# Expert gates in a two-layer block: fp16 operands that hold two tokens interleaved instead of four

## The chip, the core and the metric

The kernel runs on one core of a Trainium2 chip, in one launch. A core has TensorE (PE: matmuls; PEld is its weight load, which overlaps the matmul), VectorE (DVE), ScalarE (ACT), GpSimd (POOL) and SyncE (SP, which issues DMAs). The metric is the device time of one execution in microseconds (us); the kernel before is given by the median of three runs, and the changed one is timed in the same way. One execution of each kernel was profiled, and all rows below come from that one.

## What is computed

The program is two transformer-like blocks on 256 tokens of width 1024. The change is in the last part of the second block, a feed-forward layer with 16,384 experts (PEER). Every token has 8 heads; each head picks 16 experts out of 128 x 128 by two lists of sub-keys, and gets a softmax gate for each. Cut to what matters:

```python
T = 256; PEER_HEADS = 8; PEER_TOPK = 16; PEER_NKEYS = 128
best_s, best_j = lax.top_k(cand_s, PEER_TOPK)
idx = jnp.take_along_axis(cand_i, best_j, axis=-1)   # expert = 128 * i1 + i2
gates = jax.nn.softmax(best_s, axis=-1)

def retrieve(args):
    xc, ic, gc = args
    uc = u_tab[ic]
    vc = v_tab[ic]
    hdn = jax.nn.gelu(jnp.einsum('cd,chkd->chk', xc, uc)) * gc
    return jnp.einsum('chk,chkd->cd', hdn, vc)
```

## The kernel before

The kernel gathers nothing. It computes all 128 x 128 experts for all tokens as dense products, row by row: a row is the 128 experts with one value of i1.

- **Values of the hidden layer.** For each of 128 rows, `row` multiplies the row of `u` with the tokens. Each row of weights (512 KB) is read by a DMA on SP's queue and split in two parts (`whi` by ScalarE at line 123, `wlo` by VectorE at line 124), and a product is three matmuls (lines 183 to 185), here with 128 x 128 weights and 256 moving columns in a 4-byte type into the tile `pu`. ScalarE applies Gelu (line 1628) and leaves the result in `H`, 128 (i2) x 128 rows (i1) x 256 tokens.
- **Gates.** `H` is then multiplied by a gate that is zero for all but the 128 chosen experts of a token. `gates(g, t0)` makes these factors for 8 tokens (`G`) and for one half (`g`) of the 128 rows. With a token's 128 choices on the partitions, `b` holds a one-hot of i2 (128 wide), `e` a one-hot of the half's 64 values of i1, and `a` is `e` times the gate, in a coarse part and a remainder (`k` = 0, 1). These are fp16 tiles made by VectorE (lines 1661, 1663 and, twice, 1666). For each token two fp16 matmuls (line 1670; weights from `b`, 128 x 128; moving operand from `a`, 64 columns) add up to the 128 x 64 factors in the PSUM tile `pw`; VectorE multiplies them into `H` (line 1672). So a block of gates is 16 pairs of weight load and matmul on TensorE and five VectorE operations, and there are 2 halves x 32 groups of tokens = 64 blocks, 1,024 such matmuls in all.
- **Output.** For each of 128 rows `hs` is the split of `H` (lines 1715 and 1716), and four groups of three matmuls (lines 183 to 185, 512 moving columns) add the row of `v` into four PSUM tiles `pout`.

Four tokens lie interleaved in the fp16 tiles: the last index of `b`, `e` and `a` is the token within its group of four, so that VectorE's operations have rows of four consecutive 2-byte elements. A token's slice, which TensorE reads, is then every fourth element: its columns are 8 bytes apart, in `a` (moving operand) and in `b` (weights) alike. The constant `iob` holds each number from 0 to 127 four times, to be compared with.

The order is set by the program text: `step` puts the next block of gates behind a pair of rows when the block is due or when a budget of VectorE time allows. The first half's blocks stand among the `pu` rows, the second half's among the `pout` rows. Every engine works through its own queue in order; `b` and `a` have two buffers each, `e` one, `pw` two.

Of the kernel before, what the change touches and what calls it, by code (L numbers as in the profile page):

```python
# [23 lines left out]
F16 = mybir.dt.float16  # L24
# [3 lines left out]
OP = mybir.AluOpType  # L28
# [3 lines left out]
P = 128  # L32
# [52 lines left out]
class K:  # L85
# [1515 lines left out]
    def peer(self, out, parked_x):  # L1601
        nc, tc, d = self.nc, self.tc, self.d

        AT = (0, 64, 128)
        G = 8
        with ExitStack() as ctx:
            pool = lambda n, b, **kw: ctx.enter_context(tc.tile_pool(name=self.name(n), bufs=b, reuse_waits="tile", **kw))
            pu = pool("ppu", 2, space=PSUM)
# [4 lines left out]
            wk = pool("pwk", 2)  # L1613
            i1b = keep.tile([P, S], F16, name="i1b")
            i2b = keep.tile([P, S], F16, name="i2b")
            g2 = keep.tile([P, 2, S], F16, name="g2")
            iob = keep.tile([P, P, 4], F16, name="iob")
# [34 lines left out]

            def gates(g, t0):

                n, r0 = G // 4, AT[g]
                nr = AT[g + 1] - r0
                t4 = lambda a: a[:, t0:t0 + G].rearrange("p (n t) -> p n t", t=4)
                b = wk.tile([P, n, P, 4], F16, name=self.name("b"), tag="b")
                e = wk.tile([P, n, 64, 4], F16, name=self.name("e"), tag="e", bufs=1)[:, :, :nr]
                a = wk.tile([P, 2, n, 64, 4], F16, name=self.name("a"), tag="a")[:, :, :, :nr]  # L1660
                nc.vector.tensor_tensor(b, t4(i2b).unsqueeze(2).to_broadcast([P, n, P, 4]),
                                        iob.unsqueeze(1).to_broadcast([P, n, P, 4]), op=OP.is_equal)
                nc.vector.tensor_tensor(e, t4(i1b).unsqueeze(2).to_broadcast([P, n, nr, 4]),
                                        iob[:, r0:r0 + nr].unsqueeze(1).to_broadcast([P, n, nr, 4]), op=OP.is_equal)
                for k in range(2):
                    nc.vector.tensor_tensor(a[:, k], t4(g2[:, k]).unsqueeze(2).to_broadcast([P, n, nr, 4]), e, op=OP.mult)
                pw = self.pw.tile([P, G, 64], F32, name=self.name("pw"), tag="pw")[:, :, :nr]
                for t in range(G):
                    for k in range(2):
                        nc.tensor.matmul(pw[:, t], b[:, t // 4, :, t % 4], a[:, k, t // 4, :, t % 4], start=k == 0, stop=k == 1)  # L1670
                hv = H[:, r0:r0 + nr, t0:t0 + G]
                nc.vector.tensor_tensor(hv, pw.rearrange("p t a -> p a t"), hv, op=OP.mult)

            def work():

                for c in self.route(keep, sc, room, iob, g2, i1b, i2b):
                    yield ROUTED, c
                for g in range(len(AT) - 1):
                    for t0 in range(0, S, G):
                        yield P - 1 + AT[g], GCOST[0] + GCOST[1] * (AT[g + 1] - AT[g]) / 64  # L1680
                        gates(g, t0)
# [47 lines left out]
            g = H[:, 8:12].rearrange("p a b -> p (a b)")  # L1729
# [44 lines left out]
def _plan(start, stop):  # L1774
# [41 lines left out]
    for n, f in ((1, lambda: ffn(0, 1)), (2, nsa), (3, lambda: (ffn(0, 2), ffn(1, 1))), (4, diff),  # L1816
                 (5, lambda: ffn(1, 2)), (6, block2), (99, peer)):
        if start < n <= stop:
            f()
# [172 lines left out]
```

## Time and profile before

| | us |
|---|---|
| median of 3 runs | 2266.61 (2261.97 to 2271.68) |
| the profiled execution, device time | 2267.65 |
| its span, first to last instruction | 2265.9 |
| TensorE busy | 2214.5 (98%) |
| VectorE busy | 1643.8 (73%) |
| ScalarE busy | 1137.3 (50%) |
| mean granted TensorE clock | 0.984 of full |

The profiled execution lies 1.04 us above the median, and 1.75 us of it are outside its span. Busy time counts an engine as busy while any of its instructions is running; matmuls overlap one another, so what a matmul costs in a stream is the distance from its start to the next one's start, not its own duration. The blocks of gates run from 1666.5 to 2049.4 us of the span.

### The profile page before, as it was taken

How to read it: one execution, taken by the hardware profiler on the slowest of the kernel's cores; microseconds unless marked ns; L12 is line 12 of the kernel's file. 1: busy time of each engine (PE TensorE's matmuls, PEld its weight loads, DVE VectorE, ACT ScalarE, POOL GpSimd, SP SyncE). 2: the span in 40 equal slices, each digit the busy share in tenths (PEclk: the TensorE clock that was granted, in tenths of full speed). 3: DMA queues.
4: the chain of work that ended last, by engine and by line, in shares of the span. 5: the costliest groups of instructions: out<-in, count | busy, mean ns of one | idle time of the engine just before them, and what ended most of it. 6: DMA issues, size and time to landing. Idle time of an engine off the chain costs nothing. (4 is left out here: it accounts for less than half of the span.)

```text
span 2265.9 us, 35790 instructions
## 1 busy us (share of the span) xinstructions
PE 2214.5 (98%) x13730; PEld 1875.1 (83%) x13730; DVE 1643.8 (73%) x3303; ACT 1137.3 (50%) x1789; POOL 33.3 (1%) x75
## 2 busy tenths in 40 slices
PE   8999999999999998999999999999999999999999
PEld 7887646888788776888787777999999998888887
DVE  6867666997787587787577567896767767885555
ACT  6554575554555464655455444454533344334443
POOL 1000000000000002000000000000000000000000
PEclk9999989999999997999999999999999999999999
DMA  6654424888655442555432125445544445445554
GB/s 215 195 190 170 154 70 148 298 272 269 237 198 182 166 150 74 163 190 193 130 138 85 66 85 194 140 168 195 184 161 149 150 167 186 159 155 180 195 194 150
DMA packets 107563, 383.33 MB, mean 169 GB/s; under 512 B 13440, under 2 KB 13824, under 8 KB 107392
## 3 DMA queue, kind: packets, MB, share of 16 engines
q1 hardware_dynamic: 103392, 374.39, 48.7%
q10 hardware_dynamic: 3360, 4.55, 0.6%
q8 instruction: 108, 1.77, 0.3%
q0 software_dynamic: 640, 2.11, 0.3%
q14 instruction: 63, 0.52, 0.1%
HBM read 378.89 MB, written 2.11 MB: 168 GB/s over the span
## 5 line engine op out<-in xcount | busy, mean ns | idle before, releaser
L123 ACT ACTIVATE whi<-raw 128x1024 fp32r<-128x1024 f32 x654 | 690.7, 1059 | 767.5 <-PE pout L184 205.0
L124 DVE TENSOR_TENSOR wlo<-raw,whi 128x1024 fp32r<-128x1024 f32 x654 | 797.7, 1223 | 327.1 <-ACT whi L123 318.7
L191 PE MATMUL pair<-xx,whi 128*128 128x512 f32 x1280 | 449.8, 396 | 0.0
L192 PE MATMUL pair<-xx,wlo 128*128 128x256 f32 x1280 | 359.8, 281 | 0.0
L183 PE MATMUL pu<-xx,whi 128*128 128x256 f32 x1024 | 292.6, 286 | 1.1 <-ACT H L1628 1.1
L184 PE MATMUL pu<-xx,wlo 128*128 128x256 f32 x1024 | 290.2, 283 | 0.0
L185 PE MATMUL pu<-xx,whi 128*128 128x256 f32 x1024 | 290.1, 283 | 0.0
L191 PEld LDWEIGHTS pair<-xx,whi 128*128 128x128 f32 x1280 | 240.8, 188 | 55.7 <-issue 0.2
L192 PEld LDWEIGHTS pair<-xx,wlo 128*128 128x128 f32 x1280 | 242.7, 190 | 0.5 <-issue 0.2
L183 PE MATMUL pout<-whi,hs 128*128 128x512 f32 x512 | 201.4, 394 | 0.2 <-ACT hs L1715 0.2
L184 PE MATMUL pout<-whi,hs 128*128 128x512 f32 x512 | 199.5, 390 | 0.2 <-DVE hs L1716 0.2
L185 PE MATMUL pout<-wlo,hs 128*128 128x512 f32 x512 | 199.6, 390 | 0.0
L183 PEld LDWEIGHTS pu<-xx,whi 128*128 128x128 f32 x1024 | 197.0, 192 | 1.3 <-ACT H L1628 1.3
L184 PEld LDWEIGHTS pu<-xx,wlo 128*128 128x128 f32 x1024 | 196.5, 192 | 0.0
L185 PEld LDWEIGHTS pu<-xx,whi 128*128 128x128 f32 x1024 | 196.4, 192 | 0.0
L183 PE MATMUL pair<-whi,hT 128*128 128x512 f32 x352 | 138.5, 393 | 6.6 <-DVE x L350 6.6
L185 PE MATMUL pair<-wlo,hT 128*128 128x512 f32 x352 | 139.2, 396 | 0.0
L184 PE MATMUL pair<-whi,lT 128*128 128x512 f32 x352 | 138.3, 393 | 0.0
L183 PE MATMUL bank<-whi,xx 128*128 128x512 f32 x288 | 118.0, 410 | 1.1 <-DVE rsg L167 0.5
L184 PE MATMUL bank<-whi,xx 128*128 128x512 f32 x288 | 115.7, 402 | 0.0
L185 PE MATMUL bank<-wlo,xx 128*128 128x512 f32 x288 | 114.9, 401 | 0.0
L185 PEld LDWEIGHTS pout<-wlo,hs 128*128 128x128 f32 x512 | 96.1, 188 | 20.2
(562 smaller groups left out, 3505.5 us busy)
## 6 DMA issues: line engine op xcount, KB each, us to landing
raw<-in_pu_dram SPq DMA_DIRECT2D x128, 512.0 KB, 3.5
raw<-in_pv_dram SPq DMA_DIRECT2D x128, 512.0 KB, 3.5
raw<-in_f1i_dram SPq DMA_DIRECT2D x88, 512.0 KB, 4.1
raw<-in_f2i_dram SPq DMA_DIRECT2D x88, 512.0 KB, 4.3
araw<-in_wada_dram SPq DMA_DIRECT2D x48, 512.0 KB, 4.7
raw<-in_f1o_dram SPq DMA_DIRECT2D x44, 512.0 KB, 3.5
raw<-in_f2o_dram SPq DMA_DIRECT2D x44, 512.0 KB, 3.7
raw<-in_wi_dram SPq DMA_DIRECT2D x28, 512.0 KB, 3.4
```

Source lines behind the costliest of these rows:

```text
L123: nc.scalar.activation(hi, raw, AF.Copy)
L124: nc.vector.tensor_tensor(lo, raw, hi.bitcast(F32), op=OP.subtract)
L183: mm(out, lh, rh, start=start, stop=False)
L184: mm(out, ll, rh, start=False, stop=False)
L185: mm(out, lh, rl, start=False, stop=stop)
L191: mm(out, lh, rr, start=start, stop=False)
L192: mm(out[:, 0], ll, rr[:, 0], start=False, stop=stop)
```

## The change

A new constant `Q = 2` takes the place of the 4 in the layout: `b`, `e` and `a` hold groups of two tokens. Their sizes are the same (four groups of two instead of two groups of four for 8 tokens). A token's slice is now every second element, columns 4 bytes apart. VectorE's operations have the same number of elements, in rows of two, and read the first two of the four copies in `iob`. The matmuls are the same in number and shape.

```diff
         AT = (0, 64, 128)
         G = 8
+        Q = 2
...
-                n, r0 = G // 4, AT[g]
+                n, r0 = G // Q, AT[g]
                 nr = AT[g + 1] - r0
-                t4 = lambda a: a[:, t0:t0 + G].rearrange("p (n t) -> p n t", t=4)
-                b = wk.tile([P, n, P, 4], F16, name=self.name("b"), tag="b")
-                e = wk.tile([P, n, 64, 4], F16, name=self.name("e"), tag="e", bufs=1)[:, :, :nr]
-                a = wk.tile([P, 2, n, 64, 4], F16, name=self.name("a"), tag="a")[:, :, :, :nr]
-                nc.vector.tensor_tensor(b, t4(i2b).unsqueeze(2).to_broadcast([P, n, P, 4]),
-                                        iob.unsqueeze(1).to_broadcast([P, n, P, 4]), op=OP.is_equal)
-                nc.vector.tensor_tensor(e, t4(i1b).unsqueeze(2).to_broadcast([P, n, nr, 4]),
-                                        iob[:, r0:r0 + nr].unsqueeze(1).to_broadcast([P, n, nr, 4]), op=OP.is_equal)
+                tq = lambda a: a[:, t0:t0 + G].rearrange("p (n t) -> p n t", t=Q)
+                b = wk.tile([P, n, P, Q], F16, name=self.name("b"), tag="b")
+                e = wk.tile([P, n, 64, Q], F16, name=self.name("e"), tag="e", bufs=1)[:, :, :nr]
+                a = wk.tile([P, 2, n, 64, Q], F16, name=self.name("a"), tag="a")[:, :, :, :nr]
+                nc.vector.tensor_tensor(b, tq(i2b).unsqueeze(2).to_broadcast([P, n, P, Q]),
+                                        iob[:, :, :Q].unsqueeze(1).to_broadcast([P, n, P, Q]), op=OP.is_equal)
+                nc.vector.tensor_tensor(e, tq(i1b).unsqueeze(2).to_broadcast([P, n, nr, Q]),
+                                        iob[:, r0:r0 + nr, :Q].unsqueeze(1).to_broadcast([P, n, nr, Q]), op=OP.is_equal)
                 for k in range(2):
-                    nc.vector.tensor_tensor(a[:, k], t4(g2[:, k]).unsqueeze(2).to_broadcast([P, n, nr, 4]), e, op=OP.mult)
+                    nc.vector.tensor_tensor(a[:, k], tq(g2[:, k]).unsqueeze(2).to_broadcast([P, n, nr, Q]), e, op=OP.mult)
...
-                        nc.tensor.matmul(pw[:, t], b[:, t // 4, :, t % 4], a[:, k, t // 4, :, t % 4], start=k == 0, stop=k == 1)
+                        nc.tensor.matmul(pw[:, t], b[:, t // Q, :, t % Q], a[:, k, t // Q, :, t % Q], start=k == 0, stop=k == 1)
```

No instruction is added, removed or moved: the instructions of all engines stand in the order in which they stood, and only the line numbers behind the new line are higher by one.

## Rows read from the trace of the kernel before

**Rows 1.** The page: busy time of each engine; the chain that ended last, by line.

```profile
PE 2214.5 (98%) x13730; PEld 1875.1 (83%) x13730; DVE 1643.8 (73%) x3303; ACT 1137.3 (50%) x1789; POOL 33.3 (1%) x75
...
PE pout L183 5%; PE pout L184 5%; PE pout L185 5%; PE pu L183 5%; PE pu L184 5%; PE pu L185 5%; PE pw L1670 3%; DVE wlo L124 1%; DVE H L1524 1%; DVE H L1526 0%; DVE H L1523 0%; DVE H L1525 0%; DVE H L1522 0%; PE pq L183 0%; PE pq L184 0%
```

**Rows 2.** Busy time by stretch: gates among pu rows, then among pout rows.

```profile
core 0: us, PE busy (x) PEld busy (x) DVE busy (x) ACT busy (x) POOL busy (x), PEclk, DMA share, GB/s
1666.50:1845.00 178.50, 178.50 (x1726) 177.46 (x1725) 134.22 (x211) 66.36 (x77) 0.00 (x0) 1.00 0.44 149
1880.00:2049.40 169.40, 169.04 (x1088) 140.07 (x1086) 143.94 (x229) 67.93 (x79) 0.00 (x0) 1.00 0.49 164
```

**Rows 3.** Chain of waits from 1660 us (start, us, what) and from 1880 us.

```profile
1759.17 1.00 PE pw L1670 x16
1760.17 0.17 PE pu L183
1765.97 1.01 PE pw L1670 x16
1766.98 0.17 PE pu L183
1772.79 2.00 PE pw L1670 x32
...
1946.34 1.00 PE pw L1670 x16
1947.35 0.28 PE pout L183
1952.87 1.01 PE pw L1670 x16
1953.88 0.28 PE pout L183
```

**Rows 4.** Timeline about one block: start, us, engine, line, what [idle before].

```profile
1765.33 0.28 PE L185 MATMUL pu<-xx,whi 128*128 128x256 f32 x1
...
1765.45 0.28 PE L183 MATMUL pu<-xx,whi 128*128 128x256 f32 x1
...
1765.81 0.99 PEld L1670 LDWEIGHTS <-b 128*128 128x128 f16 x16
1765.81 1.17 PE L1670 MATMUL pw<-a,b 128*128 128x64 f16 x16
...
1766.79 0.36 PE L183 MATMUL pu<-xx,whi 128*128 128x256 f32 x1
```

**Rows 5.** The same view among the pout rows.

```profile
1948.63 0.39 PE L183 MATMUL pout<-whi,hs 128*128 128x512 f32 x1
1948.86 0.39 PE L184 MATMUL pout<-whi,hs 128*128 128x512 f32 x1
...
1949.72 0.76 DVE L1666 TENSOR_TENSOR a<-g,e 128x512 f16<-128x512 f16 x2
...
1952.71 1.17 PE L1670 MATMUL pw<-a,b 128*128 128x64 f16 x16
```

**Rows 6.** The first two weight loads of the block of rows 4.

```profile
1765.81 0.15 PEld L1670 LDWEIGHTS <-b 128*128 128x128 f16 x2
```

**Rows 7.** Instructions of the gates: min/median/max ns, first and last start.

```profile
L1670 PEld LDWEIGHTS <-b x1024: 111/117/139, 1666.5 to 2048.9; 128*128 128x128 f16 x171
L1670 PE MATMUL pw<-a,b x1024: 227/243/251, 1666.5 to 2049.0; 128*128 128x64 f16 x171
```

**Rows 8.** VectorE by line and shape, 1560 to 2265 us: xcount | busy us, mean ns | idle before.

```profile
L124 DVE TENSOR_TENSOR wlo<-raw,whi 128x1024 fp32r<-128x1024 f32 x224 | 273.9, 1223 | 156.7 <-ACT whi L123 156.7
L1666 DVE TENSOR_TENSOR a<-g,e 128x512 f16<-128x512 f16 x128 | 48.8, 420 | 0.0
L1672 DVE TENSOR_TENSOR H<-pw,H 128x512 f32<-128x512 f32 x64 | 44.1, 690 | 54.3 <-PE pw L1670 54.3
L1661 DVE TENSOR_TENSOR b<-i2b,iob 128x1024 f16<-128x1024 f16 x64 | 43.9, 686 | 1.6 <-PE pw L1670 1.6
...
L1663 DVE TENSOR_TENSOR e<-i1b,iob 128x512 f16<-128x512 f16 x64 | 27.0, 422 | 1.1
...
L1588 DVE TENSOR_TENSOR H<-H 128x1024 f16<-128x1024 f16 x2 | 1.3, 668 | 0.0
```

## The prediction

> **What bounds the kernel now.** I read the page first: TensorE is busy 98% of the span, and the chain that ended last names it for every stage of the expert layer, with 3% of the span for the fp16 matmuls of the gates [rows 1]. The change touches nothing outside 1666.5 to 2049.4 us, so the question is what sets the pace there. The table by stretch shows TensorE busy without a gap in both parts, at the full granted clock (1.00, the 2.4 GHz level), while VectorE stands idle for 178.5 - 134.2 = 44.3 us of the first part and 25.5 us of the second, and ScalarE and the DMA engines are about half busy or less [rows 2]. The chain by time says the same from block to block: about 1.00 us of gate matmuls, then at once `pu` or `pout` matmuls; a double block takes 2.00 us, exactly twice one [rows 3]. VectorE waits for TensorE at the multiply into `H` (54.3 us over the 64 blocks, 0.85 us each), not the other way round [rows 8]. So a nanosecond taken from a gate matmul is a nanosecond of the span, as long as VectorE keeps up.
>
> **What a gate matmul costs, and why.** The sixteen matmuls of a block take 1.17 us from the first start to the last end; the last alone takes 0.243 (the median), so fifteen steps take 0.927 us, 62 ns each [rows 4, 7]. That is much for 64 columns. The 4-byte matmuls around them give a scale: with 256 columns they start 0.12 us apart [rows 4], with 512 columns 0.23 us apart [rows 5], with the same 128 x 128 weights. The difference, 0.11 us for 256 columns, is 0.43 ns a column, one tick of 2.4 GHz (0.417 ns) within the rounding; 13 ns are left over for each matmul (120 - 107). By that scale 64 columns cost 27 ns and a step 40 ns at most. The measured 62 ns is 22 more. Taking off the same 13 leaves 49 ns for 64 columns, and taking off nothing leaves 62: 1.8 to 2.3 ticks a column, in place of one.
>
> Is it the weight load that takes so long? The first two loads of a block, which have nothing before them in the block to wait for, are both done after 0.15 us, and one alone takes 0.111 to 0.117 us, so the second ended 0.033 to 0.039 us after the first [rows 6, 7]. A load can thus be repeated every 36 ns or so; that is not the 62. What differs between the gate matmuls and the others is the spacing of the moving columns: 4 bytes in `pu` and `pout`, where 4-byte elements lie side by side, 8 bytes in the gates. Twice the bytes passed over for a column, about twice the time. That is the reading on which the forecast rests: moving columns 4 bytes apart stream at one tick each, columns 8 bytes apart at two.
>
> **The change part by part.** *Moving operand.* Columns are 4 bytes apart, the spacing that streams at one tick in rows 4 and 5. The step should fall from 62 ns to 27 ns plus a leftover. The leftover is 13 ns in the `pu` rows and 62 - 53 = 9 ns in the gates themselves if their columns take two ticks. That gives 36 to 40 ns. The weight load is the next bound, at some 36 ns if its own spacing makes no difference to it, so the step can't fall much below that unless loads get faster too. I take 37 ns: the load's bound and the gates' own leftover agree on 36, and 40 pulls it up a little. No row shows 2-byte elements at a 4-byte spacing, so both ends stand for the range: 27 ns with no leftover at all, and 62 ns, no change. A step above 62 I exclude: the columns lie in half as many bytes as before, and nothing else of the matmul changes.
>
> *Sum on TensorE.* Each of the 64 blocks has 15 steps inside it, 960 in all; the step from the last matmul to the next `pu` or `pout` matmul I leave as it is, because there the 4-byte weights are being loaded (that matmul takes 0.36 us where its neighbours take 0.28 [rows 4]). 960 x (62 - 37) = 24.0 us. With 40 ns it is 21.1 us, with 36 ns 25.0 us, with 27 ns 33.6 us.
>
> *Weights.* `b`'s columns come closer too. Loads lie beside the matmuls, so a faster load gives nothing beyond what is counted; it only lifts the bound of 36 ns.
>
> *VectorE.* Five operations a block, same elements. The fp16 ones run at double pace: 422 ns for 512 elements and 686 for 1024, where the 4-byte ones take 690 and 1223 [rows 8]. Do rows of two keep that pace? The nearest row is the fp16 add of line 1588 on 1024 elements, in rows of 32: 668 ns, against 686 for `b` in rows of four. Eight times as many rows cost 18 ns at most, 0.08 ns a row. Doubling them for `b`, `e` and two `a` adds 640 rows, some 50 ns a block by that, and nothing that ends the wait: VectorE idles 44.3 / 32 = 1.38 us a block in the first part (32 blocks) and 25.5 / 30 = 0.85 us in the second (30 blocks lie inside that stretch, two just before it). I count it at nothing; the cover is that idle time. A gain below nothing I don't expect from rows twice as many. If it is gone, see the last rival.
>
> *What is late next.* With blocks 15 x 25 = 0.375 us shorter, VectorE's idle time falls to about 1.0 and 0.48 us a block, and its wait for `pw` shrinks by the same 0.375 us, since the multiply into `H` is what waited. The factors of a block are ready well ahead: `a` begun at 1949.72 and done 0.76 us later belongs to the block that starts at 1952.71, 2.2 us on [rows 5]. So TensorE doesn't start to wait. The DMA share of 0.44 to 0.49 rises by a fifteenth.
>
> *Time.* 2267.65 - 24.0 = 2243.6 us for the profiled execution. That one lay 1.04 us above the median, so against the median: 2266.61 - 24.0 = 2242.6, which I call 2243 us. Differences under about 0.5% (11 us) are what a measurement of this kernel can't tell from no change.
>
> **The rivals.**
> *Partial.* The cost could go by a column's place in memory in finer steps than two and one, or a floor for a pair of load and matmul could lie between 37 and 62 ns. For: the 49 to 62 ns are not a clean two ticks, and nothing shows 2-byte elements at 4 bytes. Against: 4-byte elements at that spacing are at full pace [rows 4, 5]. With a step of 50 ns the gain is 960 x 12 = 11.5 us: 2255. [...]
>
> *No gain.* The 62 ns is a fixed price of a pair whose weights are 2-byte, or the 8-byte spacing costs nothing and the columns are not what is slow: then 2266 to 2267. For: no other 2-byte matmul stands in the trace to compare with. Against: the loads' 33 to 39 ns [rows 6, 7] and one tick a column leave no resource that is busy for 62. [...]
>
> *Slower: VectorE loses its double pace.* If operands in rows of two are taken one element at a time, `b` goes from 686 to 1223 ns and `e` and both `a` from 421 to 690, together + 1.34 us a block [rows 8]. Among the `pu` rows that fits into 1.38 us of idle time and just eats the gain. Among the `pout` rows the idle time is 0.85 us a block: VectorE becomes the bound there, and a block's period grows by 1.34 - 0.85 = 0.49 us, 30 x 0.49 = 14.7 us. That gives 2281 us, and it decides from + 0.85 us a block. Against: the rows of four and of 32 cost the same, which says that row ends are not paid for; two elements still fill a pair.
>
> **How the numbers follow.** Forecast (steps of 27 to 43 ns, 2233 to 2249): 0.65. Partial: 0.13, half of it over 0.5%. No gain: 0.16. Slower: 0.05; 0.01 is left. Faster by over 0.5%: 0.65 + 0.07 + 0.02 for a small gain that chance helps over the line = 0.74; within: 0.06 + 0.14 + 0.01 = 0.21; slower: 0.05. The range holds the forecast and the partial case: from 960 x 34 = 33 us gained (2234) to 2264, where only the no-gain and the slower case are left out.
>
> **What would show it.** In the profile after, a block's sixteen matmuls should span 0.243 + 15 x 0.037 = 0.80 us in place of 1.17, and a double block some 1.2 us on the chain in place of 2.00; `pu` and `pout` steps stay at 0.12 and 0.23 us. VectorE's four fp16 operations should keep 686 and 421 ns, within 30; its wait for `pw` should fall from 54 to about 30 us. I am wrong if the block still spans 1.1 us or more (column spacing is not the price), if TensorE shows idle time or steps over 62 ns in front of `H`'s rows, or if `b` takes over 1 us.

## The result

The changed kernel takes 2235.52 us (median of 4 runs, 2227.63 to 2239.65) against 2264.29 us for the kernel before in the runs beside it (2259.22 to 2271.68): a ratio of 0.9866, interval 0.9825 to 0.9908, some 29 us or 1.3% faster. The forecast was 24 us, 2243. The direction held, and the cause that was named is borne out by the experiments; the gain is a fifth larger than forecast, because the step between gate matmuls was put too high, and the time lies at the very edge of the range (2234 to 2264).

The profiled execution of the changed kernel has a span of 2237.8 us against 2265.9, 28.1 us less. Its lines beside those of before, first the gates' instructions by tile (min/median/max ns; first and last start), to be compared with [rows 7]:

```profile
L1671 PEld LDWEIGHTS <-b x1024: 96/97/101, 1669.0 to 2020.9; 128*128 128x128 f16 x171
L1671 PE MATMUL pw<-a,b x1024: 191/193/205, 1669.0 to 2021.0; 128*128 128x64 f16 x171
```

The stretch from the first gate matmul to the last shrank from 382.5 us (1666.5 to 2049.0) to 352.0, 30.5 us less. That is a little more than the whole gain: this execution came to the gates 2.5 us later than the one before, through stages that the change doesn't touch. The timeline about one block (start us, us, engine, line, what), to be compared with [rows 4]:

```profile
1720.97 0.28 PE L185 MATMUL pu<-xx,whi 128*128 128x256 f32 x1
1721.09 0.54 PEld L1671 LDWEIGHTS <-b 128*128 128x128 f16 x16
1721.10 0.66 PE L1671 MATMUL pw<-a,b 128*128 128x64 f16 x16
...
1721.59 0.36 PE L183 MATMUL pu<-xx,whi 128*128 128x256 f32 x1
...
1721.79 0.28 PE L184 MATMUL pu<-xx,wlo 128*128 128x256 f32 x1
```

Sixteen matmuls span 0.66 us in place of 1.17. With 0.193 us for the last alone, a step is (0.66 - 0.193) / 15 = 31 ns, where it was 62. The chain of waits shows the same, blocks of 0.50 us and double blocks of 0.99 in place of 1.00 and 2.00 [rows 3]:

```profile
1714.44 0.99 PE pw L1671 x32
1715.43 0.20 PE pu L183
1721.25 0.50 PE pw L1671 x16
1721.75 0.20 PE pu L183
```

VectorE by line and shape (xcount | busy us, mean ns | idle before), beside [rows 8]: the operations in rows of two take what the rows of four took, and the wait for `pw` has fallen from 54.3 to 30.7 us.

```profile
L1667 DVE TENSOR_TENSOR a<-g,e 128x512 f16<-128x512 f16 x128 | 48.8, 419 | 0.0
L1673 DVE TENSOR_TENSOR H<-pw,H 128x512 f32<-128x512 f32 x64 | 44.0, 689 | 30.7 <-PE pw L1671 30.7
L1662 DVE TENSOR_TENSOR b<-i2b,iob 128x1024 f16<-128x1024 f16 x64 | 43.8, 685 | 1.1 <-PE pw L1671 1.1
```

Busy time by stretch (PE, PEld, DVE, ACT, POOL, granted clock, DMA share, GB/s), beside [rows 2]: the DMA share rises from 0.44 and 0.49 to 0.51 and 0.55, twice the fifteenth that was forecast, and VectorE has 164.00 - 134.04 = 29.96 us of idle time left among the `pu` rows (32 blocks, 0.94 us each) and 153.60 - 141.88 = 11.72 among the `pout` rows (30 blocks, 0.39 us each). The forecast had 1.0 and 0.48.

```profile
1669.00:1833.00 164.00, 164.00 (x1735) 162.94 (x1734) 134.04 (x211) 66.69 (x77) 0.00 (x0) 1.00 0.51 164
1867.40:2021.00 153.60, 153.54 (x1081) 125.08 (x1081) 141.88 (x227) 66.61 (x78) 0.00 (x0) 1.00 0.55 179
```

### The profile page after: what moved, and what is told of

Its sections match the earlier page's. It is cut to its first block, busy times and chain, and to the rows that moved or that the text cites. A ratio compares the mean times of both kernels' runs of the same rounds, so it can differ in the third digit from the quotient of the medians.

```text
span 2237.8 us, 35790 instructions
## 1 busy us (share of the span) xinstructions
PE 2185.7 (98%) x13730; PEld 1846.1 (82%) x13730; DVE 1641.6 (73%) x3303; ACT 1138.1 (51%) x1789; POOL 33.4 (1%) x75
## 4 chain that ended last, share of the span: by engine, by line
PE 84%; DVE 9%; DMA 3%; ACT 2%; issue 1%; POOL 1%; ACTq 0%; SPq 0%; DVEq 0%
PE pair L191 13%; PE pair L192 7%; PE pout L183 5%; PE pout L184 5%; PE pout L185 5%; PE pu L183 5%; PE pu L184 5%; PE pu L185 5%; PE bank L183 4%; PE bank L184 4%; PE bank L185 4%; PE pair L183 4%; PE pair L184 3%; PE pair L185 3%; DVE wlo L124 3%; PE pw L1671 1%
## 5 line engine op out<-in xcount | busy, mean ns | idle before, releaser
L183 PE MATMUL pout<-whi,hs 128*128 128x512 f32 x512 | 201.2, 394 | 1.2 <-ACT hs L1716 1.2
```

Source lines behind the costliest of these rows:

```text
L183: mm(out, lh, rh, start=start, stop=False)
```

## The experiments

The change moves two operands of the same matmul closer, and both got faster: a load's own duration fell from 117 to 97 ns, a matmul's from 243 to 193. The theory (M) is that the spacing of the moving columns set the step. The first rival (W) is that the weights' spacing did; the second (S) that load and columns add up on one path, 62 = twice 31 being a suspicious halving. In all kernels below `QA` is the number of tokens interleaved in `e` and `a` (moving), `QB` that in `b` (weights). The diffs are cut to the lines that make the difference and stand against the changed kernel, where `Q` is 2 in all places.

**One half of the change at a time.** Moving operand at 4 bytes, weights left at 8:

```diff
-        Q = 2
+        QA, QB = 2, 4
```

> Only the moving operand (a, e) has two tokens interleaved (columns 4 bytes apart); the weights (b) keep four (8 bytes). Read is the step from one gate matmul to the next: 62 ns before, 31 ns with both at 4 bytes. Theory M (the moving columns' spacing is the price, two ticks a column at 8 bytes): 31 to 36 ns, the latter if a weight load at 8 bytes can only be repeated every 36 ns; 25 to 30 us faster than before, about 2236 to 2240. Rival W (the weights' spacing is the price): 62 ns and the time of before, 2264. Rival S (load and columns share one path and add up): in between, 40 to 53 ns, 2245 to 2256, and together with the other half of the change 93 ns.

Measured: 2234.87 us, ratio to the kernel before 0.9853 (0.9804 to 0.9903): the whole gain, within the noise. A block spans 0.71 us, a step is (0.71 - 0.197) / 15 = 34 ns. And the weights at 4 bytes, the moving operand left at 8:

```diff
-        Q = 2
+        QA, QB = 4, 2
```

> Only the weights (b) have two tokens interleaved (4 bytes); the moving operand (a, e) keeps four (8 bytes). M: step 58 to 62 ns and the time of before, 2261 to 2264; a load's own duration falls from 117 to 97 ns as with the whole change. W: 31 ns and the whole gain, about 2235. S: in between, 40 to 53 ns, 2245 to 2256.

Measured: 2263.74 us, ratio 1.0000 (0.9976 to 1.0025): nothing. The step is (1.14 - 0.241) / 15 = 60 ns. The gates' rows by tile and a block on the timeline, moving operand alone first:

```profile
L1671 PE MATMUL pw<-a,b x1024: 191/197/223, 1666.9 to 2022.6; 128*128 128x64 f16 x171
...
L1671 PEld LDWEIGHTS <-b x1024: 111/116/133, 1666.9 to 2022.6; 128*128 128x128 f16 x171
...
1706.23 0.71 PE L1671 MATMUL pw<-a,b 128*128 128x64 f16 x16
```

and weights alone:

```profile
L1671 PE MATMUL pw<-a,b x1024: 218/241/244, 1654.7 to 2035.6; 128*128 128x64 f16 x171
...
L1671 PEld LDWEIGHTS <-b x1024: 96/117/119, 1654.7 to 2035.6; 128*128 128x128 f16 x171
...
1711.83 1.14 PE L1671 MATMUL pw<-a,b 128*128 128x64 f16 x16
```

M holds; W and S fall, since 34 and 60 don't lie in the middle. The 34 ns are what loads at 8 bytes allow: with columns at 4 bytes in both kernels, the weights' spacing alone makes the difference between 34 and 31. One expectation of M missed: with the weights at 4 bytes beside slow columns, a load's median stays at 117 ns (96 at least). A load's recorded duration therefore holds waiting too and is no measure of the load where the columns set the pace.

**Wider spacing.** Eight tokens interleaved in the moving operand, 16 bytes from column to column (`iob` gets eight copies):

```diff
-        Q = 2
+        QA, QB = 8, 2
```

> Moving operand with eight tokens interleaved (columns 16 bytes apart), weights with two (4 bytes). M, if the price goes on with the spacing (four ticks a column): 64 x 1.67 = 107 ns, step 110 to 118 ns, 974 steps inside the groups of blocks x (114 - 62) = 51 us above the before, about 2315. M, if two ticks is the most that spacing costs: 62 ns and 2264. W: 31 ns, 2235. S: 31 ns plus three times the columns' share of 31, somewhere from 50 to 100.

Measured: 2323.37 us in its one run, and (2.03 - 0.296) / 15 = 116 ns a step: M with the price going on, four ticks a column (64 x 1.67 = 107 ns) and 9 ns over. The time is 8 us above the 2315 of the expectation, which did not have the granted clock of 0.97 in this stretch, by an estimate 13 us (see the last section). The same for the weights, 16 bytes, with the moving operand at 4:

```diff
-        Q = 2
+        QA, QB = 2, 8
```

> Weights with eight tokens interleaved (16 bytes), moving operand with two (4 bytes). M: the loads lie beside the matmuls and set the step only when they are the longer; a load's duration went from 97 to 117 ns from 4 to 8 bytes, so 140 to 160 ns here, and the step is 50 to 75 ns; time 2250 to 2275. W: step of 110 to 125 ns, about 2315. S: 31 ns plus three times the load's share, 50 to 100.

Measured: 2264.88 us in its one run, a load takes 166 ns (140 to 160 had been expected) and the step is (1.15 - 0.224) / 15 = 62 ns. M's range of 50 to 75 holds, W's 110 to 125 doesn't. So the weights' spacing has a price too, 62 ns against 116 for the moving columns at the same spacing, and it showed where the moving columns alone would have allowed 31 ns (34 ns with weights at 8 bytes, 62 at 16), not where they took 60. A load has 128 columns and a matmul here 64, so one weight column pays about a quarter of what one moving column pays (62 / 128 = 0.48 ns against 116 / 64 = 1.81). A spacing of 16 bytes in the weights alone costs as much as 8 bytes did in the moving columns.

Does the price go with the bytes passed over, or with pieces of memory that are read? At 32 bytes the two part. The tile `a` gets a pitch of 16 elements, of which eight are used, and one buffer for want of room (the diff is against the kernel with moving columns 16 bytes apart):

```diff
-                a = wk.tile([P, 2, na, 64, QA], F16, name=self.name("a"), tag="a")[:, :, :, :nr]
+                a = wk.tile([P, 2, na, 64, 2 * QA], F16, name=self.name("a"), tag="a", bufs=1)[:, :, :, :nr, :QA]
```

> As the run with the moving columns 16 bytes apart, but the tile a has a pitch of 16 elements, eight of them used, so the moving columns are 32 bytes apart; e stays at 16, the weights at 4; a has one buffer in place of two for want of room, so that VectorE may wait for TensorE between blocks. Read is the step inside a block: 31, 60 and 116 ns at 4, 8 and 16 bytes. Theory L (memory is read in pieces of 16 bytes, and a column alone in its piece is the worst case): 116 ns again. Theory B (the price goes with the bytes passed over without end): 64 x 3.33 = 213 and some 9, 222 ns. Time by L about 2320, more where the single buffer makes anyone wait; by B some 105 us more.

Measured: 2328.42 us in its one run, (2.05 - 0.299) / 15 = 117 ns a step. That is the 116 of L, and far from the 222 of B. A block on the timeline at 16 bytes, then at 32:

```profile
1701.24 2.03 PE L1671 MATMUL pw<-a,b 128*128 128x64 f16 x16
```

```profile
1704.96 2.05 PE L1671 MATMUL pw<-a,b 128*128 128x64 f16 x16
```

At spacings of 4, 8, 16 and 32 bytes the steps are 31, 60, 116 and 117 ns: the price about doubles with the spacing up to 16 bytes and stands still from there. Pieces of 16 bytes are the author's reading of these four numbers; no run shows the reads themselves. By this reading 64 columns touch 16, 32, 64 and 64 pieces of 16 bytes, and an estimate from the four steps is 29 ns for 16 more pieces, 56 for 32 more, about 1.8 ns a piece, and 3 ns over. The prediction's own words, bytes passed over, hold up to 16 bytes and no further.

**What sets the 31 ns that are left?** Both operands at 2 bytes (one token at a time):

```diff
-        Q = 2
+        QA, QB = 1, 1
```

> One token at a time: moving operand and weights both unit-spaced (2 bytes); VectorE's operations then have single elements of i1b, i2b and the gates against every fourth of iob, so they should lose their double pace: b 686 to about 1220 ns, e and both a 421 to about 690, 1.34 us a block more. Theory T (a column takes one tick at least, two ticks at 8 bytes, and the spacing below 4 bytes gives nothing): gate step stays at 29 to 31 ns. Rival B (the price is bytes passed over, all the way down): 15 to 20 ns. For the time: the change left VectorE about 0.9 us of idle time a block among the pu rows and 0.4 among the pout rows; 1.34 us more makes it the bound in both, 32 x 0.43 + 30 x 0.96 = 43 us above the changed kernel, about 2278, slower than the kernel before. If row ends or single elements cost VectorE nothing: 2235.

Measured: 2278.99 us, ratio to the kernel before 1.0068 (1.0051 to 1.0084), slower, close to the 2278 expected. By the estimate in pieces a step would take 17 ns (8 x 1.8 and 3); on the timeline fifteen matmuls that start without a gap have a step of (0.61 - 0.193) / 14 = 30 ns, so that price ends before 2 bytes. The author's estimate of the floor is the columns' own tick, which the trace of the kernel before gives as (227 - 120) / 256 = 0.418 ns a column: the median steps are 227 ns in the `pout` rows (512 columns) and 120 in the `pu` rows (256), at a granted clock of 1.00. 64 columns are 27 ns by it, and at 4 bytes the two limits would meet. VectorE did lose its double pace, 1218 ns for `b` in place of 685:

```profile
L1662 DVE TENSOR_TENSOR b<-i2b,iob x64: 1212/1218/1226, 1595.3 to 2052.9; 128x1024 f16<-128x1024 f16 x64
...
L1671 PE MATMUL pw<-a,b x1024: 189/193/277, 1665.4 to 2060.2; 128*128 128x64 f16 x171
```

That the time came out as expected is in part luck. Some 14 us more were expected among the `pu` rows and 29 among the `pout` rows. The rows below (from the first gate matmul to the first `pout` matmul, and from there to the last gate matmul) are 201.2 and 193.6 us long, against 198.4 and 153.6 in the changed kernel: 3 and 40 us more. TensorE is idle for 193.60 - 171.05 = 22.5 us of the second, and its mean granted clock there is 0.94 in place of 1.00, which by an estimate (0.06 x 193.6) is another 12 us that the expectation did not have.

```profile
1665.40:1866.60 201.20, 199.99 (x2034) 197.03 (x2032) 187.46 (x224) 82.80 (x97) 0.00 (x0) 1.00 0.51 165
1866.60:2060.20 193.60, 171.05 (x1083) 132.60 (x1084) 180.37 (x226) 67.48 (x78) 0.00 (x0) 0.94 0.45 144
```

With half the columns (the 128 rows in four parts of 32, so twice as many gate matmuls; both operands at 4 bytes):

```diff
-        AT = (0, 64, 128)
+        AT = (0, 32, 64, 96, 128)
```

> The 128 rows in four parts of 32 instead of two of 64, both operands at 4 bytes: twice as many blocks and gate matmuls, each with 32 moving columns and the same 128 x 128 weights. Only the step between gate matmuls is read. If the columns set the step of 31 ns (64 x 0.417 = 27 and 4 left over): 32 columns take 13 ns and the step falls to 17 to 22 ns, or to the next bound, the load. If a fixed price of a pair of load and matmul sets it: it stays at 31 ns. The time rises, since b is made twice as often (64 more blocks x some 2.2 us of VectorE).

Measured: 2319.78 us in its one run, and a step of (0.57 - 0.176) / 15 = 26 ns. The step falls, so it was no fixed price of a pair that made the 31; but by 5 ns, not by 13, to a bound that the expectation put too low; so this run does not confirm a tick a column for the gate matmuls. Whether the load at 4 bytes or a floor of the matmul is that bound of 26 ns stays open. An estimate speaks against the load: from 34 ns at 8 bytes and 62 at 16, a load at 4 bytes would take some 20 if its price goes in the same way (28 ns more for 8 bytes more, so 14 less for 4 bytes less).

**VectorE's cover.** The last rival of the prediction was a VectorE that loses its double pace. The changed kernel, but `b` and `e` read one copy in `iob` again and again, with the same results:

```diff
-                                        iob[:, :, :QB].unsqueeze(1).to_broadcast([P, nb, P, QB]), op=OP.is_equal)
+                                        iob[:, :, :1].unsqueeze(1).to_broadcast([P, nb, P, QB]), op=OP.is_equal)
...
-                                        iob[:, r0:r0 + nr, :QA].unsqueeze(1).to_broadcast([P, na, nr, QA]), op=OP.is_equal)
+                                        iob[:, r0:r0 + nr, :1].unsqueeze(1).to_broadcast([P, na, nr, QA]), op=OP.is_equal)
```

> The changed kernel, but iob is read with one copy of each number again and again instead of two copies side by side, in b and e alone; results and TensorE's operands are the same. If this takes VectorE's double pace: b 685 to about 1220 ns, e 422 to about 690, 0.80 us a block more. TensorE's step stays at 31 ns. Among the pu rows that fits into the idle time left (about 0.9 us a block); among the pout rows 0.4 us a block are left and TensorE has to wait: 30 x 0.4 = 12 us above the changed kernel, about 2247. If VectorE's idle time were no cover at all: 64 x 0.8 = 51 us, 2286; if b and e keep their pace: 2235.

Measured: 2249.3 us, ratio to the kernel before 0.9936 (0.9914 to 0.9959), 14 us above the changed kernel. `b` takes 1218 ns and `e` 684, 0.80 us a block; TensorE's gate matmuls keep their 193 ns at the median. The idle time was cover for most of the 51 us, as reckoned: stretches of the same length (columns as above) show TensorE busy without a gap among the `pu` rows and waiting among the `pout` rows. The size came out near the 12 us expected, but not by waits alone: TensorE's idle time in the second stretch is 169.00 - 163.96 = 5 us, and the clock of 0.97 over 169 us is, by an estimate, another 5.

```profile
1666.00:1835.00 169.00, 169.00 (x1776) 167.93 (x1775) 158.24 (x213) 68.66 (x79) 0.00 (x0) 1.00 0.51 165
1880.00:2049.00 169.00, 163.96 (x1077) 128.41 (x1076) 159.35 (x217) 66.91 (x77) 0.00 (x0) 0.97 0.50 163
```

## What the prediction had right, and which term failed

- **TensorE bounds the stretch, and a nanosecond of a gate matmul is one of the span.** Right: 30.5 us fell out of the stretch where TensorE's steps account for 31.2 (below).
- **The columns' spacing is the price.** Right, by the two halves of the change: 0.9853 for the moving operand alone, 1.0000 for the weights alone. "Two ticks at 8 bytes, one at 4" fits 60 and 31 ns, with 4 to 7 ns over (a tick is 0.418 ns in the trace, as above, or 2.4 columns in a ns; the traces give the clock itself as a share of full, 1.00 here, and not in GHz). The reason that was given, the bytes passed over for a column, is too simple: 16 and 32 bytes cost the same (116 and 117 ns), and 2 bytes hardly less than 4 (30 and 31).
- **A step of 37 ns.** This is the step of the prediction that failed: the term of its sum was put too high, and the measured step is 31. Two of its parts were off. The bound of 36 ns from the loads was read from loads at 8 bytes, and the text said it would hold unless loads get faster too; they did. With the weights left at 8 bytes the step is indeed 34, and with both operands at 4 it is 31. And the leftover was taken from the 4-byte matmuls (13 ns) and from 62 - 53 (9 ns); at the narrow spacing it is 31 - 27 = 4 ns.
- **960 steps.** Slightly too few. Of the 64 blocks 14 follow another block directly, so that 974 steps lie between two gate matmuls (start by start in the traces, 61.8 ns on average before and 30.9 after). The other 50 steps, from a block's last matmul to the next `pu` or `pout` matmul, were left as they were because the 4-byte weights are loaded there. They shrank too, from 47 ns to 28 at the median; the longer matmul behind them is the same 0.36 us. So 974 x (62 - 31) = 30.2 us and 50 x 0.019 = 1.0 us make 31.2, against 24.0. Of the 7.2 us between, the size of the step is 974 x (37 - 31) = 5.8.
- **What is late next.** Nothing within the blocks, as said, but one place was missed: at the passage from `pu` to `pout` rows TensorE now waits for the first `hs`, in one wait of 1.2 us that was 0.2 us before. ScalarE makes that tile after the last Gelu, whose end the shorter gates don't bring forward: the first `pout` matmul starts 2.4 us after the last `pu` matmul in both kernels (1878.07 to 1880.51 us before, 1865.03 to 1867.46 after), and the double block of gates between them fills less of that time. The prediction had not looked at that place; it takes back about 1 us of the 31.2. The wait on the timeline, before and after, and in the list of waits of the changed kernel (engine, line waited for: us, times, longest):

```profile
1880.51 1.18 PE L183 MATMUL pout<-whi,hs 128*128 128x512 f32 x4 [0.16 <-ACT hs L1715]
...
1867.46 1.19 PE L183 MATMUL pout<-whi,hs 128*128 128x512 f32 x4 [1.16 <-ACT hs L1716]
...
PE pout L183 <- ACT hs L1716: 1.2, 1, 1.2
```

- **VectorE at nothing.** Right: 685 ns for `b`, 419 and 422 for `a` and `e`. The 50 ns a block that the row ends might have cost did not come.
- **The rivals.** No gain: excluded by the runs with one half each. Partial: the step is 31 ns, so no floor lay between 37 and 62. Slower: did not happen, but the price is real; made to happen in part (`b` 1218 ns, `e` 684) it cost 14 us, and in full, with single elements (`a` 684 too), it turned the gain into a loss (1.0068).

## What to carry to other kernels

Look at the step between matmuls, not at their duration, and compare it with the columns times the time of one, as other matmuls of the same trace give it (0.418 ns here, at a granted clock of 1.00): 62 ns for 64 columns was over twice that, with weight loads that could follow one another every 34 ns (the run with the weights left at 8 bytes), and it was the moving operand's layout. Moving columns 4 bytes apart took 31 ns a step here and hardly less at 2 bytes (30); at 8 bytes they took 60. When tokens are interleaved for VectorE's sake, try how few will do: two kept the pace of both engines (31 ns a step, 685 ns for `b`), one lost VectorE's double pace (30 and 1218), four halved TensorE's (62 and 686).

## What the runs showed of the hardware that was not expected

- **Wider is not always worse.** Moving columns 32 bytes apart cost as much as columns 16 bytes apart (117 and 116 ns a step).
- **The weights pay less.** At 16 bytes 128 weight columns bound the step at 62 ns, where 64 moving columns bound it at 116.
- **VectorE pays for wide spacing too.** Where `iob` has eight copies and two of them are read, its pairs lie 16 bytes apart instead of 8. `b` then took 1083 ns in place of 684 (moving columns at 16 bytes), and `e` 623 in place of 422 (weights at 16 bytes). TensorE was idle for less than 0.5 us between the first and the last gate matmul in either kernel, so the steps above don't come from it.

```profile
L1662 DVE TENSOR_TENSOR b<-i2b,iob 128x1024 f16<-128x1024 f16 x64 | 69.3, 1083 | 2.4 <-PE pw L1671 2.4
```

```profile
L1664 DVE TENSOR_TENSOR e<-i1b,iob 128x512 f16<-128x512 f16 x64 | 39.9, 623 | 1.1
```

- **The clock can fall in these stretches.** In the kernel with one token at a time TensorE waited for VectorE among the `pout` rows, and the granted clock, 1.00 throughout that part of the changed kernel, was 0.94 on average, and 0.79 in seven of the 27 stretches of 8 us from 1850 to 2066 us. Two of them, one after the other (columns as above): TensorE idle for 2.5 us in one, mean clock 0.79 in the next.

```profile
1914.00:1922.00 8.00, 5.48 (x39) 4.24 (x37) 7.91 (x12) 2.64 (x3) 0.00 (x0) 1.00 0.50 150
1922.00:1930.00 8.00, 8.00 (x43) 5.83 (x44) 6.58 (x10) 2.18 (x3) 0.00 (x0) 0.79 0.22 76
```

Nor does it take waits: in the kernel with moving columns 16 bytes apart the clock fell as well, to 0.97 on average from the first gate matmul to the last, although TensorE was busy without a gap; 0.03 x 446.7 us is, by an estimate, 13 us of that kernel's time. What makes it fall no run shows.

```profile
1657.90:2104.60 446.70, 446.70 (x3113) 415.74 (x3112) 317.96 (x450) 150.43 (x174) 0.00 (x0) 0.97 0.42 137
```
